# FFN 1 of a hybrid encoder layer: the gates' SwiGLU in two steps, two weight sums on VectorE, the bias table written by row pieces

## The chip, the cores and the metric

The kernel runs on one core of a Trainium2 chip. The metric is device time in microseconds, the median over executions of the whole kernel. The engines are named as the profile names them: PE is TensorE's matmul and PEld its weight load, DVE is VectorE, ACT is ScalarE, POOL is GpSimd, SP is SyncE, which here only issues DMAs. Each engine works through its own instructions in the order in which they were written; between engines semaphores hold an instruction back until what it reads is there, and until what it overwrites is no longer needed.

## What is computed

One layer, for 512 tokens of width 1024, in float32:

```python
f = swiglu(rms_norm(h, ffn1_pre_g), ffn1_w1, ffn1_w3, ffn1_w2)   # (silu(x @ w1) * (x @ w3)) @ w2, d_ff 2816
h = h + 0.5 * rms_norm(f, ffn1_post_g)
u = rms_norm(h, mix_pre_g)
q, k, v, xr, xg = split(u @ w_in)
y_a = (rg_lru(causal_conv(xr)) * gelu(xg)) @ w_lru_out           # recurrent branch
y_b = swa_sink_attention(q, k, v, sinks, bias) @ w_attn_out      # windowed attention, relative bias per head
h = h + rms_norm((g0 * y_a + g1 * y_b) @ w_o, mix_post_g)        # g = sigmoid(u @ w_gate + b_gate)
y = h + 0.5 * rms_norm(swiglu(rms_norm(h, ffn2_pre_g), ffn2_w1, ffn2_w3, ffn2_w2), ffn2_post_g)
```

The bias is one table of 32 buckets by 16 heads, spread over 383 relative positions. The change touches FFN 1, one helper that FFN 2 uses too, and the place where the bias table is prepared.

## The kernel before

**Numbers in two parts.** Every float32 operand of a matmul is split into a rounded part and a rest: `whi` by a ScalarE copy (line 193 or 158), `wlo` by a VectorE subtraction (line 194 or 159). A product is then three matmuls, hi by hi, lo by hi, hi by lo.

**FFN 1.** The activations are transposed, features on partitions, and held as `uT` (hi and lo). The two weight matrices w1a and w3a are cut into 22 tiles of 128 output features each. The first four gates (a gate is one w1a tile, its partner a w3a tile) are *single* tiles: `mm_feat` runs 24 matmuls of 512 columns into a whole PSUM bank. As the RMS scale of the input is not known early, FFN 1 multiplies with the unscaled input, and the gate is scaled afterwards by `Rb`, a row of factors per token. `swiglu(f)` does all of it in `silu_mul` (lines 430 to 439): VectorE multiplies the gate's bank by `Rb` (line 436), ScalarE takes the silu (437), VectorE multiplies by the partner's bank (438). Where these run is given by a small list of due points: `later(n, fn)` puts fn at the n-th `point()` from now, and a point comes every 12 matmuls; `point(True)` runs all that is left.

**Pairs.** The other 18 gates are taken two by two in a Winograd scheme (`class Pairs`): two weight tiles together are a 2 by 2 block matrix, the input likewise, and seven block products of 12 matmuls with 256 columns (`mm_s`, lines 475 to 477) do what eight would. A *job* is one such pair of tiles; jobs alternate between w1a (the gates) and w3a (their partners), 18 jobs in FFN 1 (n = 0 to 17) and 20 in FFN 2. Four weight sums S1 to S4 are needed per job. In `prep(m, 0)` GpSimd makes all four as additions of 128 by 512, `s12` (lines 521, 522) and `s34` (523, 524); for the very first two jobs VectorE makes them (argument `dve`). `prep(m, 1)` to `prep(m, 4)` split the raw tile, S1/S2, S3/S4 and the block a22.

**A job's order** (`run`, lines 538 to 608): product a11 into bank bu and copy q1 (554); s1 into bx and copy q5 (557); then `last()`, which is the seventh product a22 of the job before; `prep(n+1, 1)`; s2 added into bu and copy u (563); `prep(n+1, 2)`; a12 into bc and an addition (572); s4 added into bx and an addition (577); `prep(n+1, 3)`; s3 added into bu, copy v (581) and an addition (582); for a w3a job the products of gate and partner (587, 588); `prep(n+1, 4)`; `prep(n+2, 0)`; the loads for job n+3. In FFN 1 `last()` of a w1a job ends with a copy (596), the scaling by `Rb` (597) and the silu (598); of a w3a job with one product (605). In FFN 2 the input is scaled beforehand, so the silu is taken at once (600 to 602). In the last job the product a12 comes after v, and `tail()` runs ahead of it: it splits the first two hidden tiles and the first two tiles of w2a, the next matrix.

**Hooks.** `late` is a table (job, place): [functions], called after q1 (place 1), q5 (2) or u (3) of that job.

**Bias.** `bias_in` loads the one-hot matrix and the table by two GpSimd DMAs; `bias_rows` makes 16 rows (one a head) of 383 values with a matmul and a ScalarE copy into `erow`; `bias_spread(i)` writes to a scratch in DRAM 128 copies of each row of two heads, 383 KB, one DMA of GpSimd's queue, eight in all. The attention reads the scratch much later (line 1038).

**Memory.** All large tiles share 42 slots of 4 KB per partition. A load on SP's queue (line 143) waits until its slot's last reader is done.

Of the kernel before, what the change touches and what calls it, by code (L numbers as in the profile page):

```python
# [13 lines left out]
ALU = mybir.AluOpType  # L14
# [37 lines left out]
def hybrid_layer(ctx: ExitStack, tc: tile.TileContext, a: dict, out: bass.AP):  # L52
# [93 lines left out]
    def dma_to(n):  # L146
        while st["dma"] < min(n, len(order)):
            dma_one(st["dma"])
            st["dma"] += 1
# [277 lines left out]
        dma_to(st["split"] + 3)  # L427


    def silu_mul(ps1, ps3, R=None):  # L430

        t = slot([P, 2, SEQ], name="sw")
        if R is None:
            act.activation(t[:, 0, :], ps1, AF.Silu)
        else:
            dve.tensor_tensor(out=t[:, 0, :], in0=ps1, in1=R, op=ALU.mult)
            act.activation(t[:, 0, :], t[:, 0, :], AF.Silu)
        dve.tensor_tensor(out=t[:, 1, :], in0=ps3, in1=t[:, 0, :], op=ALU.mult)
        return t[:, 1, :]

# [39 lines left out]
    class Pairs:  # L480
# [14 lines left out]
        def prep(self, m, i, eng=None):  # L495
            if m >= len(self.jobs) or (m, i) in self.ready:
                return
            self.ready.add((m, i))
            k = self.k0 + 2 * m
            if i == 0:  # L500
                if k not in loaded or k + 1 not in loaded:
                    self.raws(m)
                s12, s34 = slot([P, 2 * QH], name="S12"), slot([P, 2 * QH], name="S34")
                self.w[m] = {"r": (raws.pop(k), raws.pop(k + 1)), "s": (s12, s34)}
            W = self.w[m]
            (ra, rb), (s12, s34) = W["r"], W["s"]
# [12 lines left out]
            if i == 0:  # L519
                e = eng or pool  # L520
                e.tensor_tensor(out=s12[:, :QH], in0=a21, in1=a22, op=ALU.add)
                e.tensor_tensor(out=s12[:, QH:], in0=s12[:, :QH], in1=a11, op=ALU.subtract)
                e.tensor_tensor(out=s34[:, QH:], in0=a12, in1=s12[:, QH:], op=ALU.subtract)
                e.tensor_tensor(out=s34[:, :QH], in0=a11, in1=a21, op=ALU.subtract)
            elif i == 1:
                halves(both(ra), "a11", "a12")
            elif i == 2:
                halves(both(s12), "s1", "s2")
            elif i == 3:
                halves(both(s34), "s3", "s4")  # L530
            elif i == 4:
                t = slot([P, 2, QH], F32R, name="w22")
                split2(t[:, 0, :], t[:, 1, :], a22)
                W["a22"] = t[:, 0, :], t[:, 1, :]
            if all((m, x) in self.ready for x in range(5)):
                del W["r"], W["s"]

        def run(self, tail, hooks={}):
            X = self.X
            assert st["get"] == st["split"] == self.k0, (st, self.k0)  # L540
            st["get"] = st["split"] = self.k0 + 2 * len(self.jobs)
            last = lambda: None
            for n, (nm, f) in enumerate(self.jobs):
                W = self.w.pop(n)
                first = nm == self.na
                tmp = slot([P, 4, 256], name="ct")
                q1, q5, u, v = (tmp[:, i, :] for i in range(4))
                c = slot([P, 2, SEQ], name="cc")
                if first:
                    self.c1[f] = c  # L550
                bu, bx, bc = (bank("c")[:, :256] for _ in range(3))
                at = lambda i: [f() for f in hooks.get((n, i), ())]
                mm_s(W["a11"], X["b11"], bu)
                act.activation(q1, bu, AF.Copy)  # L554
                at(1)
                mm_s(W["s1"], X["t1"], bx)
                act.activation(q5, bx, AF.Copy)
                at(2)
                last()
                self.prep(n + 1, 1)  # L560
                mm_s(W["s2"], X["t2"], bu, True)
                del W["s1"], W["s2"]
                act.activation(u, bu, AF.Copy)
                at(3)
                if n == len(self.jobs) - 1:
                    tail()
                self.prep(n + 1, 2)

                def c11():
                    mm_s(W["a12"], X["b21"], bc)  # L570
                    del W["a11"], W["a12"]
                    dve.tensor_tensor(out=c[:, 0, :256], in0=bc, in1=q1, op=ALU.add)

                if n < len(self.jobs) - 1:
                    c11()
                mm_s(W["s4"], X["b22"], bx, True)
                dve.tensor_tensor(out=c[:, 0, 256:], in0=bx, in1=u, op=ALU.add)
                self.prep(n + 1, 3)
                mm_s(W["s3"], X["t3"], bu, True)
                del W["s3"], W["s4"]  # L580
                act.activation(v, bu, AF.Copy)
                dve.tensor_tensor(out=c[:, 1, 256:], in0=v, in1=q5, op=ALU.add)
                if n == len(self.jobs) - 1:
                    c11()
                if not first:
                    c1 = self.c1[f]
                    dve.tensor_tensor(out=c1[:, 0, :], in0=c1[:, 0, :], in1=c[:, 0, :], op=ALU.mult)
                    dve.tensor_tensor(out=c1[:, 1, 256:], in0=c1[:, 1, 256:], in1=c[:, 1, 256:], op=ALU.mult)
                self.prep(n + 1, 4)
                self.prep(n + 2, 0)  # L590
                self.raws(n + 3)

                def last(W=W, bu=bu, c=c, f=f, first=first):
                    mm_s(W.pop("a22"), X["t4"], bu, True)
                    if first and self.R is not None:
                        act.activation(c[:, 1, :256], bu, AF.Copy)
                        dve.tensor_tensor(out=c, in0=c, in1=self.R, op=ALU.mult)  # L597
                        act.activation(c, c, AF.Silu)
                    elif first:
                        act.activation(c[:, 1, :256], bu, AF.Silu)  # L600
                        act.activation(c[:, 0, :], c[:, 0, :], AF.Silu)
                        act.activation(c[:, 1, 256:], c[:, 1, 256:], AF.Silu)
                    else:
                        c1 = self.c1.pop(f)
                        dve.tensor_tensor(out=c1[:, 1, :256], in0=bu, in1=c1[:, 1, :256], op=ALU.mult)
                        self.hid.f += [c1[:, 0, :], c1[:, 1, :]]

            last()
# [89 lines left out]
    def t_split(n):  # L698
        X1[f"t{n + 1}"] = to_slots(tg[n])
# [37 lines left out]
        act.activation(erow[0], pse[:N_HEADS, : NREL + 1], AF.Copy)  # L737

    def bias_spread(i):
        ev = erow[0][2 * i : 2 * i + 2, :NREL]  # L740
        pool.dma_start(out=scr[2 * i : 2 * i + 2], in_=bass.AP(tensor=ev.tensor, offset=ev.offset, ap=[ev.ap[0], [0, P], ev.ap[1]]))

# [45 lines left out]
    def single(nm, i, ahead):  # L788
        w = get(nm, i, ahead=ahead)
        ps.append(bank("f"))  # L790
        mm_feat(ps[-1], w)

    def swiglu(f):
        hid.f.append(silu_mul(ps[2 * f], ps[2 * f + 1], Rb[:, 0, :]))

    X1.update((b, uview(*q)) for b, q in (("b11", (0, 0)), ("b21", (1, 0)), ("b22", (1, 1))))
    P_ = pairs_a.prep
    for n, fn in (
        (1, lambda: t_sum(0)), (1, lambda: t_split(0)), (2, lambda: t_sum(1)),
        (3, lambda: P_(0, 0, dve)), (3, lambda: t_split(1)), (3, squares), (4, root),  # L800
        (5, lambda: P_(0, 1)), (5, lambda: t_sum(2)), (6, factor), (6, lambda: swiglu(0)), (6, lambda: dma_to(pairs_a.k0 + 4)),
        (7, lambda: t_sum(3)), (7, lambda: t_split(2)), (8, lambda: P_(0, 2)), (8, lambda: swiglu(1)),
        (9, lambda: P_(0, 3)), (9, lambda: P_(0, 4)), (10, lambda: t_split(3)), (10, lambda: swiglu(2)),
        (10, lambda: P_(1, 0, dve)),
    ):
        later(n, fn)
# [8 lines left out]
    point(True)  # L815
    xg.clear()
    tg.clear()
    swiglu(3)
    late = {(6, 1): [bias_in], (9, 1): [bias_rows]}

    def w2_ahead():
        hid.to(1)
# [467 lines left out]
```

## Time and profile before

| | us |
|---|---|
| median of 3 runs | 1169.75 (1169.62 to 1171.74) |
| the profiled execution | 1168.26 |
| its span, first to last instruction | 1166.2 |

| stretch of the span, us | what runs | length | PE busy | DVE busy | ACT busy | POOL busy | granted clock |
|---|---|---|---|---|---|---|---|
| 0 to 61 | FFN 1, single tiles | 61.0 | 51.67 | 43.36 | 39.34 | 6.16 | 0.96 |
| 61 to 251.3 | FFN 1, pairs | 190.3 | 184.38 | 156.54 | 97.17 | 118.77 | 0.99 |
| 251.3 to 367 | last product of the pairs, w2a | 115.7 | 102.49 | 55.48 | 44.26 | 2.19 | 0.94 |
| 367 to 834 | norms, projections, both branches, merge | 467.0 | 466.95 | 323.32 | 264.40 | 104.96 | 1.00 |
| 834 to 1039 | FFN 2, pairs | 205.0 | 205.00 | 168.50 | 112.63 | 127.93 | 1.00 |
| 1039 to 1166.2 | w2b, last norm, output | 127.2 | 120.51 | 52.25 | 37.70 | 0.56 | 0.98 |

How to read what follows. A timeline row gives the start in us from the span's beginning, the duration, the engine, the line, the operation, the tiles written and read, and in brackets how long the engine had been idle and what released it. A wait row gives who waited for whom, the total, how often, and the longest. A group row gives a count, the total busy time, the mean of one in ns, and the idle time before. A row of stretches gives for each engine its busy time and, after x, its number of instructions, then the granted TensorE clock (1.00 is full), the busy share of the 16 DMA engines, and GB/s.

### The profile page before, as it was taken

The page shows a single profiled execution, that of the slowest core. Times are in us where ns is not written, and L with a number is a line of the kernel's source. Part 1 is how long each engine was busy: PE and PEld are TensorE (multiplying, and loading weights), DVE is VectorE, ACT ScalarE, POOL GpSimd, SP SyncE. Part 2 cuts the span into 40 slices and gives each one's busy share as a digit, 9 for nine tenths or more (in the row PEclk, how much of TensorE's full clock was granted, in tenths as well). Part 3 has the DMA queues.
Part 4 walks back from the last instruction along what each step waited for, and adds up shares of the span by engine and source line. Part 5 has one row for each costly group of instructions (what it writes and reads, how often), then busy time and mean ns, then how long its engine had stood idle before and what let it go on. Part 6 is the DMA issues. An engine that isn't in the chain of part 4 may idle for free.

```text
span 1166.2 us, 17529 instructions
## 1 busy us (share of the span) xinstructions
PE 1131.0 (97%) x6835; PEld 1010.4 (87%) x6835; DVE 799.4 (69%) x1180; ACT 595.5 (51%) x1060; POOL 360.6 (31%) x275
## 2 busy tenths in 40 slices
PE   9889999969999999999999999999999999999997
PEld 7789999857888987788888888888999999998886
DVE  5868889845834765678586865767899778875313
ACT  7554554534523536983465654346555555564211
POOL 0046766530000000000455655000676557700000
PEclk9989999989999999999999999999999999999999
DMA  9213223279621521223332324360232333255101
GB/s 339 78 57 106 105 80 108 73 116 210 200 90 73 199 73 55 73 91 98 101 91 73 93 72 144 97 210 29 81 109 82 102 108 109 91 167 169 62 19 54
DMA packets 41873, 125.00 MB, mean 107 GB/s; under 512 B 9344, under 2 KB 11136, under 8 KB 41792
## 3 DMA queue, kind: packets, MB, share of 16 engines
q1 hardware_dynamic: 34272, 115.15, 29.9%
q0 software_dynamic: 7376, 8.49, 4.0%
q8 instruction: 53, 0.87, 0.3%
q10 hardware_dynamic: 144, 0.26, 0.1%
q14 instruction: 28, 0.23, 0.1%
HBM read 116.50 MB, written 7.33 MB: 106 GB/s over the span
## 4 chain that ended last, share of the span: by engine, by line
PE 80%; DVE 7%; DMA 5%; ACT 5%; issue 2%; SPq 0%; DVEq 0%; ACTq 0%
PE f L204 9%; PE f L203 9%; PE f L205 9%; PE c L475 8%; PE c L476 8%; PE c L477 8%; PE acc L223 8%; PE acc L221 8%; PE acc L222 8%; DVE wlo L194 3%; DMA raw_w2a<-in_w2a_dram 2%; ACT whi L193 1%; DVE cc L597 1%; PE pt L1093 1%; DMA raw_w3a<-in_w3a_dram 1%
## 5 line engine op out<-in xcount | busy, mean ns | idle before, releaser
L203 PE MATMUL f<-uT,whi 128*128 128x512 f32 (+1 forms) x472 | 171.9, 364 | 0.0
L204 PE MATMUL f<-uT,wlo 128*128 128x512 f32 (+1 forms) x472 | 170.7, 362 | 0.1
L205 PE MATMUL f<-uT,whi 128*128 128x512 f32 (+1 forms) x472 | 170.4, 361 | 0.0
L475 PE MATMUL c<-Xh,whi 128*128 128x256 f32 x456 | 131.0, 287 | 11.8 <-ACT ct L554 8.6
L223 PE MATMUL acc<-whi,hT 128*128 128x512 f32 x352 | 137.3, 390 | 0.3 <-DVE hT L194 0.3
L221 PE MATMUL acc<-whi,hT 128*128 128x512 f32 x352 | 137.5, 391 | 0.0
L222 PE MATMUL acc<-wlo,hT 128*128 128x512 f32 x352 | 137.1, 390 | 0.0
L476 PE MATMUL c<-Xh,wlo 128*128 128x256 f32 x456 | 130.3, 286 | 1.6 <-DVE wlo L194 1.6
L476 PE MATMUL c<-uT,wlo 128*128 128x256 f32 x456 | 129.8, 285 | 0.0
L475 PE MATMUL c<-uT,whi 128*128 128x256 f32 x456 | 129.8, 285 | 0.0
L477 PE MATMUL c<-Xl,whi 128*128 128x256 f32 x456 | 129.7, 285 | 0.0
L477 PE MATMUL c<-uT,whi 128*128 128x256 f32 x456 | 129.6, 284 | 0.0
L194 DVE TENSOR_TENSOR wlo<-S,whi 128x1024 fp32r<-128x1024 f32 x76 | 120.8, 1590 | 4.4 <-ACT whi L193 4.2
L203 PEld LDWEIGHTS f<-uT,whi 128*128 128x128 f32 x472 | 89.2, 189 | 14.5 <-issue 1.4
L204 PEld LDWEIGHTS f<-uT,wlo 128*128 128x128 f32 x472 | 89.3, 189 | 13.7 <-DVE wlo L159 0.9
L205 PEld LDWEIGHTS f<-uT,whi 128*128 128x128 f32 x472 | 89.2, 189 | 13.5
L475 PEld LDWEIGHTS c<-Xh,whi 128*128 128x128 f32 x456 | 88.0, 193 | 14.7 <-ACT ct L554 10.2
L476 PEld LDWEIGHTS c<-Xh,wlo 128*128 128x128 f32 x456 | 88.1, 193 | 2.6 <-DVE wlo L194 2.6
L476 PEld LDWEIGHTS c<-uT,wlo 128*128 128x128 f32 x456 | 88.2, 193 | 0.2 <-DVE wlo L194 0.2
L475 PEld LDWEIGHTS c<-uT,whi 128*128 128x128 f32 x456 | 88.2, 194 | 0.0
L477 PEld LDWEIGHTS c<-Xl,whi 128*128 128x128 f32 x456 | 88.1, 193 | 0.0
L477 PEld LDWEIGHTS c<-uT,whi 128*128 128x128 f32 x456 | 88.1, 193 | 0.0
(316 smaller groups left out, 2743.6 us busy)
## 6 DMA issues: line engine op xcount, KB each, us to landing
raw_w2a<-in_w2a_dram SPq DMA_DIRECT2D x22, 512.0 KB, 15.9
raw_w1b<-in_w1b_dram SPq DMA_DIRECT2D x22, 512.0 KB, 4.1
raw_w3b<-in_w3b_dram SPq DMA_DIRECT2D x22, 512.0 KB, 4.2
raw_w2b<-in_w2b_dram SPq DMA_DIRECT2D x22, 512.0 KB, 4.4
raw_w3a<-in_w3a_dram SPq DMA_DIRECT2D x21, 512.0 KB, 4.4
raw_w1a<-in_w1a_dram SPq DMA_DIRECT2D x20, 512.0 KB, 4.3
raw_wg<-in_wg_dram SPq DMA_DIRECT2D x16, 512.0 KB, 3.7
raw_xr<-in_xr_dram SPq DMA_DIRECT2D x8, 512.0 KB, 4.1
```

The source lines that it names most:

```text
L193: act.activation(hi, src, AF.Copy)
L194: dve.tensor_tensor(out=lo, in0=src, in1=f32(hi), op=ALU.subtract)
L203: pe.matmul(ps[:, c0:c1], wh[:, s], h_, start=k == 0, stop=False)
L204: pe.matmul(ps[:, c0:c1], wl[:, s], h_, start=False, stop=False)
L205: pe.matmul(ps[:, c0:c1], wh[:, s], l_, start=False, stop=k == KT - 1)
L221: pe.matmul(acc[n], x[:, 0, c], wh[:, s], start=first, stop=False)
L222: pe.matmul(acc[n], x[:, 0, c], wl[:, s], start=False, stop=False)
L223: pe.matmul(acc[n], x[:, 1, c], wh[:, s], start=False, stop=last)
L475: pe.matmul(ps, wh[:, s], xh, start=first, stop=False, skip_group_check=True)
L476: pe.matmul(ps, wl[:, s], xh, start=False, stop=False, skip_group_check=True)
L477: pe.matmul(ps, wh[:, s], xl, start=False, stop=k == 3, skip_group_check=True)
L597: dve.tensor_tensor(out=c, in0=c, in1=self.R, op=ALU.mult)
```

## The change

- `silu_mul` is cut in two. `gate(f)` does the scaling by `Rb` on VectorE, `swiglu(f)` the silu and the product. For gates 0 and 1 they stand one point apart (the scalings at points 6 and 7, the rest at 7 and 8). Gate 2 is scaled at point 10 and finished in job 0 after q1; gate 3, which stood ahead of the pairs, is scaled in job 0 after u and finished in job 1 after q1.
- In the pairs of FFN 1 `last()` no longer takes the silu of the scaled gates itself but hands it back, and `run` issues it ahead of the product s3: the products s2, a12 and s4 stand between.
- S3 and S4 are made by VectorE in `prep(m, 2)`, ahead of the split of S1/S2, in place of `prep(m, 0)`, where GpSimd (VectorE for the first two jobs) made them. This holds for both FFNs.
- `bias_in` moves from job 6 to job 1, `bias_rows` from job 9 to job 3. `bias_spread` writes 16 copies for all 16 heads in place of 128 copies for two heads, still 383 KB each and eight in all, and they move from points of the w2a product into jobs 4 to 11, one a job, after q1.

```diff
-    def silu_mul(ps1, ps3, R=None):
+    def silu_mul(ps1, ps3, t=None):
-        t = slot([P, 2, SEQ], name="sw")
-        if R is None:
-            act.activation(t[:, 0, :], ps1, AF.Silu)
-        else:
-            dve.tensor_tensor(out=t[:, 0, :], in0=ps1, in1=R, op=ALU.mult)
-            act.activation(t[:, 0, :], t[:, 0, :], AF.Silu)
+        t = t or slot([P, 2, SEQ], name="sw")
+        act.activation(t[:, 0, :], ps1, AF.Silu)
         dve.tensor_tensor(out=t[:, 1, :], in0=ps3, in1=t[:, 0, :], op=ALU.mult)
...
                 e.tensor_tensor(out=s12[:, QH:], in0=s12[:, :QH], in1=a11, op=ALU.subtract)
-                e.tensor_tensor(out=s34[:, QH:], in0=a12, in1=s12[:, QH:], op=ALU.subtract)
-                e.tensor_tensor(out=s34[:, :QH], in0=a11, in1=a21, op=ALU.subtract)
             elif i == 1:
                 halves(both(ra), "a11", "a12")
             elif i == 2:
+                dve.tensor_tensor(out=s34[:, QH:], in0=a12, in1=s12[:, QH:], op=ALU.subtract)
+                dve.tensor_tensor(out=s34[:, :QH], in0=a11, in1=a21, op=ALU.subtract)
                 halves(both(s12), "s1", "s2")
...
-                last()
+                silu = last() or silu
                 self.prep(n + 1, 1)
...
                 self.prep(n + 1, 3)
+                silu()
+                silu = lambda: None
                 mm_s(W["s3"], X["t3"], bu, True)
...
                         dve.tensor_tensor(out=c, in0=c, in1=self.R, op=ALU.mult)
-                        act.activation(c, c, AF.Silu)
-                    elif first:
+                        return lambda: act.activation(c, c, AF.Silu)
+                    if first:
...
-        ev = erow[0][2 * i : 2 * i + 2, :NREL]
-        pool.dma_start(out=scr[2 * i : 2 * i + 2], in_=bass.AP(tensor=ev.tensor, offset=ev.offset, ap=[ev.ap[0], [0, P], ev.ap[1]]))
+        ev, rows = erow[0][:, :NREL], slice(16 * i, 16 * i + 16)
+        pool.dma_start(out=scr[:, rows, :], in_=bass.AP(tensor=ev.tensor, offset=ev.offset, ap=[ev.ap[0], [0, 16], ev.ap[1]]))
...
+    gates = {}
+    def gate(f):
+        gates[f] = slot([P, 2, SEQ], name="sw")
+        dve.tensor_tensor(out=gates[f][:, 0, :], in0=ps[2 * f], in1=Rb[:, 0, :], op=ALU.mult)
     def swiglu(f):
-        hid.f.append(silu_mul(ps[2 * f], ps[2 * f + 1], Rb[:, 0, :]))
+        t = gates.pop(f)
+        hid.f.append(silu_mul(t[:, 0, :], ps[2 * f + 1], t))
...
-    swiglu(3)
-    late = {(6, 1): [bias_in], (9, 1): [bias_rows]}
+    late = {(0, 1): [lambda: swiglu(2)], (0, 3): [lambda: gate(3)], (1, 1): [bias_in, lambda: swiglu(3)], (3, 1): [bias_rows]}
+    for i in range(P // 16):
+        late[4 + i, 1] = [lambda i=i: bias_spread(i)]
...
-    for i in range(N_HEADS // 2):
-        later(4 + 3 * i, lambda i=i: bias_spread(i))
```

More of the change, by code (lines that the diff above doesn't have):

```diff
@@ L541, in run @@
             st["get"] = st["split"] = self.k0 + 2 * len(self.jobs)
-            last = lambda: None
+            last = silu = lambda: None
             for n, (nm, f) in enumerate(self.jobs):
@@ L800, in hybrid_layer @@
         (3, lambda: P_(0, 0, dve)), (3, lambda: t_split(1)), (3, squares), (4, root),
-        (5, lambda: P_(0, 1)), (5, lambda: t_sum(2)), (6, factor), (6, lambda: swiglu(0)), (6, lambda: dma_to(pairs_a.k0 + 4)),
-        (7, lambda: t_sum(3)), (7, lambda: t_split(2)), (8, lambda: P_(0, 2)), (8, lambda: swiglu(1)),
-        (9, lambda: P_(0, 3)), (9, lambda: P_(0, 4)), (10, lambda: t_split(3)), (10, lambda: swiglu(2)),
+        (5, lambda: P_(0, 1)), (5, lambda: t_sum(2)), (6, factor), (6, lambda: gate(0)), (7, lambda: swiglu(0)), (6, lambda: dma_to(pairs_a.k0 + 4)),
+        (7, lambda: t_sum(3)), (7, lambda: t_split(2)), (8, lambda: P_(0, 2)), (7, lambda: gate(1)), (8, lambda: swiglu(1)),
+        (9, lambda: P_(0, 3)), (9, lambda: P_(0, 4)), (10, lambda: t_split(3)), (10, lambda: gate(2)),
         (10, lambda: P_(1, 0, dve)),
```

## The prediction

> **What bounds the kernel now.** First the span, then TensorE's own waits, then the stretches around them, and last the engines that end them.
>
> ```profile
> core 0: 1166.2 us, clock 0.988
> ```
> ```profile
> PE 1131.0 (97%) x6835; PEld 1010.4 (87%) x6835; DVE 799.4 (69%) x1180; ACT 595.5 (51%) x1060; POOL 360.6 (31%) x275
> ```
> ```profile
> PE c L475 <- ACT ct L581: 12.9, 1, 12.9
> PE c L475 <- ACT ct L554: 8.6, 4, 7.6
> PE c L475 <- ACT ct L563: 3.3, 6, 1.2
> PE c L476 <- DVE wlo L194: 1.6, 5, 0.5
> ```
>
> TensorE is busy 97% of the span, so only its idle time can be won. Its longer waits (total, times, longest) all stand on the products of `mm_s`: two of 12.9 and 7.6 us, and a dozen short ones. A gap also costs clock, so each stretch is counted by its matmuls (x is their number; the last three columns are granted clock, DMA share and GB/s):
>
> ```profile
> 53.40:61.00 7.60, 0.09 (x1) 0.00 (x0) 6.14 (x8) 1.50 (x4) 5.33 (x4) 0.65 0.34 132
> 61.00:73.50 12.50, 12.42 (x85) 12.42 (x86) 5.94 (x8) 5.19 (x10) 3.23 (x3) 0.80 0.13 42
> 73.50:245.00 171.50, 165.88 (x1348) 162.11 (x1347) 147.08 (x144) 88.28 (x145) 115.54 (x68) 1.00 0.29 92
> 251.30:264.20 12.90, 0.07 (x1) 0.00 (x0) 0.45 (x2) 1.32 (x2) 0.00 (x0) 0.59 0.93 162
> 264.20:279.00 14.80, 14.42 (x62) 12.08 (x63) 6.53 (x11) 3.17 (x5) 1.07 (x1) 0.89 0.94 206
> 300.00:323.00 23.00, 23.00 (x103) 19.05 (x102) 18.48 (x20) 15.45 (x19) 0.00 (x0) 1.00 0.53 168
> 861.00:1029.00 168.00, 168.00 (x1403) 168.00 (x1402) 138.58 (x146) 90.22 (x158) 104.19 (x62) 1.00 0.30 100
> ```
>
> The FFN 2 pairs (last row) run without a gap: 168.00/1403 = 0.120 us for a matmul of 256 columns, so a job of 84 takes 10.06. From 300 to 323 one of 512 columns takes 23.00/103 = 0.223. Against these rates FFN 1 loses time in three places:
> - start of the pairs: 7.6 idle, then 85 matmuls in 12.5 where 10.2 would do, 2.3 more at a clock of 0.80. Together 9.9.
> - 16 jobs from 73.5 to 245: 171.5 less 1346 × 0.1197 = 161.1, and less an estimated 1.0 for the two other matmuls (the bias rows): 9.4.
> - end of the pairs: 12.9 idle, then 12 + 50 matmuls in 14.8 where 1.4 + 11.2 would do, 2.2 more at 0.89. Together 15.1.
>
> That is 34.4 us, all that can be won here. The Trainium skill (TensorE: Matmul & The Clock Gate, "Part 1: The HAM clock gate") puts the time at half clock after a restart at about 3.4 us, an estimated 1.7 lost each time. These rows show 2.3 and 2.2; by the page the 34.4 would be 1.1 less.
>
> **Start: the gates' SwiGLU.** ScalarE, then VectorE, then GpSimd before the 7.6 us wait ends (start, duration, line, tiles, idle before):
>
> ```profile
> 53.48 0.63 ACT L437 ACTIVATE sw<-sw 128x512 f32<-128x512 f32 x1 [2.16 <-DVE sw L436]
> 60.13 0.63 ACT L437 ACTIVATE sw<-sw 128x512 f32<-128x512 f32 x1 [6.02 <-DVE sw L436]
> 60.66 0.36 ACT L554 ACTIVATE ct<-c 128x256 f32<-128x256 f32 x1
> ```
> ```profile
> 49.88 1.22 DVE L194 TENSOR_TENSOR wlo<-S,whi 128x1024 fp32r<-128x1024 f32 x1 [0.26 <-ACT whi L193]
> ...
> 54.75 0.68 DVE L521 TENSOR_TENSOR S<-raw_w3a 128x512 f32<-128x512 f32 x1
> 55.46 0.69 DVE L522 TENSOR_TENSOR S<-S,raw_w3a 128x512 f32<-128x512 f32 x1
> 56.19 1.63 DVE L523 TENSOR_TENSOR S<-raw_w3a,S 128x512 f32<-128x512 f32 x1
> 57.75 1.74 DVE L524 TENSOR_TENSOR S<-raw_w3a,raw_w3a 128x512 f32<-128x512 f32 x1
> 59.41 0.68 DVE L436 TENSOR_TENSOR sw<-f,Rb 128x512 f32<-128x512 f32 x1
> ```
> ```profile
> 55.52 1.76 POOL L521 TENSOR_TENSOR S<-raw_w1a 128x512 f32<-128x512 f32 x1 [54.07 <-DVE S L521]
> ```
>
> Job 0's third product adds into bank bu, so it waits for the copy q1 (L554). On ScalarE that copy stands behind gate 3's silu, which waits for its scaling (59.41), which stands on VectorE behind the four adds for job 1. The change puts q1 ahead: gate 2's silu comes behind q1, gate 3's scaling behind u, its silu behind q1 of job 1. Of the four adds two stay here. So q1 runs when its product ends and the 9.9 go. What is late next is job 1's second product, which needs wlo of S1/S2. VectorE's queue to it, from 53.45 (where the scaling ends that releases the silu of 53.48): two adds 0.68 + 0.69, the SwiGLU product 0.69, wlo of the raw tile 1.22, gate 3's scaling 0.68, S4 and S3 1.37, wlo 1.22: 60.0, and with GpSimd's two adds alongside (1.63 and 1.74 against 0.68 shows about 1 us per collision) up to 62. TensorE asks for it five products (four of job 0, one of job 1, 12 × 0.12 = 1.44 each) after 53.4, at 60.6. So the new wait is between 0 and 1.5; I take 1.5, since GpSimd's row at 55.52 falls right among VectorE's. **Term: 8.4 won**, bounds 5 (another pair of collided adds, 3.4, in front) and 9.9.
>
> **The pairs' silu and S3/S4.** VectorE's groups from 73.5 to 245, and ScalarE's silu:
>
> ```profile
> L194 DVE TENSOR_TENSOR wlo<-S,whi 128x1024 fp32r<-128x1024 f32 x32 | 54.0, 1688 | 0.9 <-ACT whi L193 0.9
> L582 DVE TENSOR_TENSOR cc<-ct 128x256 f32<-128x256 f32 x16 | 19.8, 1237 | 0.0
> ...
> L572 DVE TENSOR_TENSOR cc<-c,ct 128x256 f32<-128x256 f32 x16 | 6.6, 414 | 0.0
> ```
> ```profile
> L598 ACT ACTIVATE cc<-cc 128x1024 f32<-128x1024 f32 x8 | 8.5, 1060 | 15.1 <-DVE cc L597 15.1
> ```
>
> Every second job ScalarE stands idle 15.1/8 = 1.9 us for the scaling L597, then does 1.06 of silu, with the next weights' whi and the copy u queued behind it; hence the waits on L563 (3.3) and on wlo (1.6). With the silu three products later both orders are free: 4.9 won. The rest of the 9.4 stays, among it 1.0 on L554 (8.6 − 7.6).
>
> Against this VectorE takes two adds a job: 2 × 0.69 = 1.38 if alone, 1.63 + 1.74 = 3.37 if GpSimd is in the way. It also gets relief, since GpSimd's adds halve: wlo takes 1.69 against 1.22 alone, L582 1.24 against 0.41 for the same shape in L572, so collisions cost 15.0 + 13.2 us in these two groups, 1.8 a job; half is 0.9. Net +0.5 on 147.08/16 = 9.2 a job, under the 10.06. What is queued behind: ScalarE's whi of S3/S4 now waits for VectorE's adds, and behind it the deferred silu, the copy v and the next q1. v is needed only two products (2.9 us) after S3 ends, so I charge 0.5 over the whole stretch, bounds 0 and 13 (in half the jobs the adds at 3.37 with this relief: 9.2 + 2.5 = 11.7, 1.6 over, 8 times). **Term: 4.4 won**, bounds 8 lost and 9.4 won. FFN 2 has the same two adds, and its silu is not scaled, so it is not deferred: 138.58/16.7 = 8.3 a job plus 0.5, still under 10.06, so nothing; bound 7 lost (8.3 + 2.5 = 10.8, 0.7 over, in half of 20 jobs). If VectorE's slack there were gone, all of the 1.38 would show in each job.
>
> On GpSimd two adds and, in eight jobs, one DMA issue are left in place of four adds. On SP's queue a load waits for a free slot, and the raw tiles are now held until VectorE's adds have read them, behind wlo of the same job instead of the job before; the loads keep a job's lead, so I charge nothing.
>
> **The end: the bias table's writes.** ScalarE around the long wait, then GpSimd's issues, then landing times (min, median, max) of the bias writes and of the w2a loads, then a load that GpSimd issues:
>
> ```profile
> 246.86 1.06 ACT L598 ACTIVATE cc<-cc 128x1024 f32<-128x1024 f32 x1 [1.29 <-DVE cc L597]
> 247.83 0.36 ACT L563 ACTIVATE ct<-c 128x256 f32<-128x256 f32 x1
> 248.09 0.62 ACT L193 ACTIVATE hT<-sw 128x512 fp32r<-128x512 f32 x1
> 248.61 1.05 ACT L158 ACTIVATE whi<-raw_w2a 128x1024 fp32r<-128x1024 f32 x1
> 249.56 0.62 ACT L193 ACTIVATE hT<-sw 128x512 fp32r<-128x512 f32 x1
> 262.88 1.06 ACT L158 ACTIVATE whi<-raw_w2a 128x1024 fp32r<-128x1024 f32 x1 [12.70 <-DMA raw_w2a<-in_w2a_dram]
> 263.84 0.36 ACT L581 ACTIVATE ct<-c 128x256 f32<-128x256 f32 x1
> ```
> ```profile
> 237.07 7.42 POOL L741 DMA_DIRECT2D bias_scr<-erow  x7
> ```
> ```profile
> DMA to landing us min/median/max: 27.9/43.2/47.8
> ```
> ```profile
> DMA to landing us min/median/max: 3.6/15.9/31.3
> ```
> ```profile
> bc_ffn_post_g<-in_ffn_post_g_dram POOLq DMA_DIRECT2D x2, 512.0 KB, 4.2
> ```
>
> The copy v (L581) frees the bank for the last a22 product, and waits behind the second whi of w2a, whose load came late: seven bias writes were issued just before, and while they ran w2a loads took a median 15.9 us where 3.6 is possible. With the writes in jobs 4 to 11 the load is there in time. ScalarE then has this queue without the silu of 246.86 in front, which comes behind it: the row of 249.56 ends at 250.2 − 1.06 = 249.1, the second whi at 250.2, the silu at 251.3 and v at 251.6. TensorE comes free at 251.3, so 0.3 is left; I charge 0.6. **Term: 14.5 won**, bounds 10 (a load that starts one landing of 4.2 too late) and 15.1.
>
> Where they go, the eight writes meet the pairs' loads, at a DMA share of 0.29. Each moves 383 KB, and none landed in under 27.9 us from 2 source partitions. From 16, its price lies between that and the 4.2 of a 512 KB load on the same queue; eight times the source rows puts it near the latter, well inside a job of 10.06. The raw tiles have a job's lead over it, so nothing shows: 0 lost here, and the dear end of the price is a rival below. The Trainium skill (DMA: Bandwidth & Descriptors, "Why a DMA increments its semaphore by 16 and not by 1") says that a copy runs on the largest number of engines up to 16 that divides the outer dimensions of both sides: 2 before, 16 after, an estimated 27.9 × 2/16 = 3.5 us. By the page too the loss is 0. The issues (1.06 each on GpSimd), the two loads and the bias rows only move.
>
> **Sum.** 8.4 + 4.4 + 14.5 = 27.3. The profiled execution took 1168.26 us (span 1166.2 and 2.1 around it), so 1141.0; the median of the runs is 1.5 above it, so I forecast 1142 (1138 to 1147).
>
> **Rivals.**
> - All three losses go: 1168.3 − 34.4 + 1.5 = 1135.4. For it: FFN 2 pairs have no gap with the same work. Against: FFN 1 has the scaling besides.
> - The pairs win nothing, the start half: 5 + 14.5 − 1 = 18.5, so 1151. For it: VectorE's 9.2 of 10.06 leaves little room, and every wlo of S pays for a collision (1.69 against 1.22).
> - The long wait stays, because w2a's loads lacked slots rather than bandwidth: 1142 + 14.5 = 1156 to 1157. Against: DMA share 0.93 in that very row.
> - Slower: VectorE becomes the bound. Adds at 3.37 without relief make 12.6 a job in FFN 1 and 11.7 in FFN 2, so 18 × 2.5 + 20 × 1.6 = 77 over the 1135.4: 1212. It decides for a loss from a net 2.2 us a job on (8.7 mean to 10.06, and 34.4/38 more); I expect 0.5.
> - Slower: the bias writes stay at 27.9 us among the pairs' loads. At w2a's 15.9 for loads with a lead of 10.7 (171.5/16) eight jobs lose 5 each, 40 on the forecast: 1182. It decides from a landing above the lead, 10.7.
>
> **Numbers.** Forecast 0.50, all gone 0.15, pairs win nothing 0.20, wait stays 0.05, VectorE bound 0.03, bias writes 0.03, other new waits, from 1154 up to a small loss, 0.04. Range: the first three, 1134 to 1154. 0.2% (2.3 us) is about what runs can tell from no change: faster 0.92 (the first four and half of the last), within 0.2% 0.02, slower 0.06.
>
> **What would show it.** Right: no gap of 7 us after job 0's second product, the first L437 in the pairs behind an L554; bias_scr landing in about 4 us and raw_w1a unchanged; w2a landing near 4; VectorE's wlo of S below 1.69; FFN 2 pairs without gaps. Wrong: waits of TensorE on L563, L581 or wlo of over 1 us in most jobs (the adds' place), raw tiles landing above 10 us, or a time above 1154.

## The result, and the profile after

| | us | runs | ratio to before, with 95% interval |
|---|---|---|---|
| before, in the same set | 1170.63 | 1169.62 to 1171.74 | |
| changed kernel | 1136.91 | 1136.39 to 1137.54 | 0.9712 [0.9695, 0.9729] |
| its profiled execution | 1137.54 | span 1135.5 | |

The kernel is 2.9% faster. The time lies inside the range of 1134 to 1154, but under the 1138 to 1147 that the likeliest case had to itself: it stands 1.5 from the rival "all three losses go" and 5.1 from the forecast.

The cores, the busy times and TensorE's waits on other engines' results (total, times, longest) of the changed kernel:

```profile
core 0: 1135.5 us, clock 0.998
```
```profile
PE 1125.4 (99%) x6835; PEld 1006.0 (89%) x6835; DVE 790.0 (70%) x1252; ACT 597.8 (53%) x1060; POOL 241.1 (21%) x203
```
```profile
PE c L472 <- DVE wlo L194: 0.6, 1, 0.6
PE c L471 <- ACT ct L579: 0.3, 1, 0.3
```

Of the waits on `mm_s` (now lines 471 to 473) the 12.9, 7.6, 3.3 and 1.6 us of before are gone; 0.6 and 0.3 are left. The granted clock rose from 0.988 to 0.998: the pairs now read 1.00 from their start, where the two stretches behind the long gaps read 0.80 and 0.89 before. The stretches that answer to the pairs of FFN 1 and FFN 2 before, with the same columns:

```profile
62.10:233.00 170.90, 170.52 (x1408) 168.93 (x1409) 152.24 (x185) 93.40 (x153) 67.20 (x38) 1.00 0.47 117
...
820.00:988.00 168.00, 168.00 (x1401) 167.84 (x1400) 129.96 (x172) 92.19 (x158) 58.76 (x32) 1.00 0.31 98
```

Counted as in the prediction: in the pairs 170.90, less 1406 × 0.1199 = 168.6 (0.1199 is 168.00/1401, the second row), less an estimated 1.0 for the bias rows' two matmuls, leaves 1.3 lost, where it was 9.4. At the end only the wait on the copy v (now L579) is lost, 0.3 where it was 15.1. At the start these rows of TensorE show the one wait that is left:

```profile
61.06 0.28 PE L471 MATMUL c<-Xh,whi 128*128 128x256 f32 x1
61.93 0.39 PE L472 MATMUL c<-Xh,wlo 128*128 128x256 f32 x1 [0.59 <-DVE wlo L194]
```

From one matmul to the next 0.87 in place of 0.12: about 0.8 lost, where it was 9.9. Together 34.4 fell to 2.4, so 32.0 were won. The two spans differ by 1166.2 − 1135.5 = 30.7. Of the 1.3 between them 0.6 is in the FFN 2 pairs, by the first and last start of their L475 (before) and L471 (after):

```profile
L475 PE MATMUL c<-uT,whi x240: 282/284/284, 838.0 to 1037.8; 128*128 128x256 f32 x120
```
```profile
L471 PE MATMUL c<-uT,whi x240: 283/283/283, 806.4 to 1006.8; 128*128 128x256 f32 x120
```

That is 199.8 before and 200.4 after. The runs below show where it comes from: the same count gives 200.3 or 200.4 in b_s34, a_silu_now, a_late_place and a_two_heads, in which VectorE makes S3 and S4 beside GpSimd's S1 and S2, and 199.8 in b_bias, b_gate, b_silu, a_s34_pool, a_mixed and a_all_dve, in which one engine makes all four in FFN 2. The other 0.7 was not followed.

### The profile page after: what moved, and what is told of

Its sections match the earlier page's. It is cut to its first block, busy times and chain, and to the rows that moved or that the text cites. A ratio compares the mean times of both kernels' runs of the same rounds, so it can differ in the third digit from the quotient of the medians.

```text
span 1135.5 us, 17456 instructions
## 1 busy us (share of the span) xinstructions
PE 1125.4 (99%) x6835; PEld 1006.0 (89%) x6835; DVE 790.0 (70%) x1252; ACT 597.8 (53%) x1060; POOL 241.1 (21%) x203
## 4 chain that ended last, share of the span: by engine, by line
PE 91%; DVE 5%; ACT 3%; issue 1%; DMA 0%; SPq 0%; DVEq 0%; ACTq 0%
PE c L472 10%; PE f L203 10%; PE f L204 10%; PE f L205 10%; PE c L473 10%; PE c L471 10%; PE acc L222 8%; PE acc L223 8%; PE acc L221 8%; DVE wlo L194 2%; PE pt L1097 1%; PE s L1061 1%; PE s L1060 1%; DVE S L523 1%; PE tr L313 1%
## 5 line engine op out<-in xcount | busy, mean ns | idle before, releaser
L471 PE MATMUL c<-Xh,whi 128*128 128x256 f32 x456 | 129.1, 283 | 0.0
L471 PE MATMUL c<-uT,whi 128*128 128x256 f32 x456 | 129.0, 283 | 0.0
L193 ACT ACTIVATE whi<-S 128x1024 fp32r<-128x1024 f32 x76 | 80.2, 1057 | 53.0 <-DVE S L523 53.0
L194 DVE TENSOR_TENSOR wlo<-S,whi 128x1024 fp32r<-128x1024 f32 x76 | 101.9, 1341 | 0.3 <-ACT whi L193 0.3
L203 PEld LDWEIGHTS f<-uT,whi 128*128 128x128 f32 x472 | 89.1, 189 | 14.5 <-issue 1.4
L204 PEld LDWEIGHTS f<-uT,wlo 128*128 128x128 f32 x472 | 89.2, 189 | 13.8 <-DVE wlo L159 0.9
L471 PEld LDWEIGHTS c<-Xh,whi 128*128 128x128 f32 x456 | 87.5, 192 | 0.6 <-ACT ct L550 0.6
L471 PEld LDWEIGHTS c<-uT,whi 128*128 128x128 f32 x456 | 87.5, 192 | 0.0
```

Of the source, the lines that this page charges most:

```text
L193: act.activation(hi, src, AF.Copy)
L194: dve.tensor_tensor(out=lo, in0=src, in1=f32(hi), op=ALU.subtract)
L203: pe.matmul(ps[:, c0:c1], wh[:, s], h_, start=k == 0, stop=False)
L204: pe.matmul(ps[:, c0:c1], wl[:, s], h_, start=False, stop=False)
L471: pe.matmul(ps, wh[:, s], xh, start=first, stop=False, skip_group_check=True)
```

## The experiments

### Each part alone

The change has four parts that can be made one at a time on the kernel before: the bias table's writes, the gates' SwiGLU in two steps, the pairs' silu, and the sums S3 and S4.

```diff
# b_bias: bias_in, bias_rows and bias_spread as in the changed kernel, nothing else
-        ev = erow[0][2 * i : 2 * i + 2, :NREL]
+        ev, rows = erow[0][:, :NREL], slice(16 * i, 16 * i + 16)
...
+        late[4 + i, 1] = [lambda i=i: bias_spread(i)]
```

> The kernel before with the bias part alone (row pieces, jobs 4 to 11). Theory, the bias writes starve the w2a loads and nothing else at the end of the pairs: TensorE's wait of 12.9 us on the copy v and its clock cost go, some 14.6 us, so 1156; the 7.6 us wait at the start and the short ones in the pairs stay; w2a lands in about 4.4 us. Rival, w2a's loads lacked slots: the long wait stays, 1169 to 1171.

Measured: 1152.68 against 1169.16 before, ratio 0.9861 [0.9846, 0.9876], 16.5 us won. TensorE's waits on the pairs' products, and w2a's loads with their median landing at the end of the row:

```profile
PE c L475 <- ACT ct L554: 8.9, 1, 8.9
PE c L476 <- DVE wlo L194: 3.5, 8, 1.1
PE c L475 <- ACT ct L563: 1.5, 4, 0.5
```
```profile
raw_w2a<-in_w2a_dram SPq DMA_DIRECT2D x22, 512.0 KB, 4.3
```

The 12.9 us wait on the copy v is gone, w2a lands in a median 4.3 where it took 15.9, and the two other losses stay. So w2a's loads did not lack slots. The 15.1 that were counted for the end lie inside the interval, which is 14.5 to 18.0 us.

```diff
# b_gate: gate(f) and swiglu(f) as in the changed kernel, nothing else
...
-    swiglu(3)
-    late = {(6, 1): [bias_in], (9, 1): [bias_rows]}
+    late = {(0, 1): [lambda: swiglu(2)], (0, 3): [lambda: gate(3)], (1, 1): [lambda: swiglu(3)], (6, 1): [bias_in], (9, 1): [bias_rows]}
```

> The kernel before with the gates' SwiGLU in two steps alone; S3 and S4 of job 1 still stand on VectorE ahead of it. Theory, the 7.6 us wait is q1 behind the silu on ScalarE: it goes though VectorE's four adds stay, 1161 to 1163. Rival, the adds themselves are what is late: a wait of 3 to 5 us comes a product later, 1165 to 1168.

Measured: 1158.66, ratio 0.9916 [0.9899, 0.9933], 10.5 us won. Its waits:

```profile
PE c L471 <- ACT ct L577: 12.8, 1, 12.8
PE c L471 <- ACT ct L559: 2.6, 5, 1.2
PE c L472 <- DVE wlo L194: 1.9, 6, 0.5
...
PE c L471 <- ACT ct L550: 1.0, 3, 0.3
```

The 7.6 us wait on q1 (L550 here) is gone; what is left on that line is the 1.0 of the later jobs. No wait longer than 1.2 takes its place, so the whole 9.9 is won (the interval is 7.8 to 11.8). That is more than the expectation's 6 to 8, which had the wait of 7.6 but not the 2.3 that the prediction counted behind it.

```diff
# b_silu: the silu of a scaled pair of gates ahead of s3 in place of behind its scaling
-                last()
+                silu = last() or silu
...
+                silu()
+                silu = lambda: None
...
-                        act.activation(c, c, AF.Silu)
+                        return lambda: act.activation(c, c, AF.Silu)
```

> The kernel before with the pairs' silu three products later alone. Theory, ScalarE's order: TensorE's waits on u (L563 before, 3.3 us) and on wlo (1.6) go, 4 to 5 us, 1166. Rival, VectorE's collisions with GpSimd set those waits: under 2 us, 1169 to 1171.

Measured: 1160.48, ratio 0.9927 [0.9910, 0.9943], 8.7 us won (6.7 to 10.5), where the prediction's sum had 4.9 for the silu and the expectation 4 to 5. TensorE's long waits on the pairs' products, and a stretch of 158 us of the pairs:

```profile
PE c L475 <- ACT ct L583: 13.8, 1, 13.8
PE c L475 <- ACT ct L554: 7.4, 1, 7.4
```
```profile
73.00:231.00 158.00, 158.00 (x1313) 157.23 (x1313) 148.16 (x141) 88.26 (x141) 112.27 (x65) 1.00 0.32 98
```

Of the waits in the pairs only the two long ones are left, and between them TensorE runs without a gap at its full rate, 158.00/1313 = 0.120 us. The silu's place alone was the cause of all that the pairs lost, also of what the wait rows had put on L554 and of the short gaps that no row named. How it reaches that far shows in one job of w1a, first before, then with the silu deferred:

```profile
95.06 2.01 DVE L597 TENSOR_TENSOR cc<-cc,Rb 128x1024 f32<-128x1024 f32 x1 [1.74 <-ACT cc L596]
...
97.10 1.06 ACT L598 ACTIVATE cc<-cc 128x1024 f32<-128x1024 f32 x1 [2.07 <-DVE cc L597]
98.06 1.04 ACT L193 ACTIVATE whi<-raw_w1a 128x1024 fp32r<-128x1024 f32 x1
...
99.01 0.36 ACT L563 ACTIVATE ct<-c 128x256 f32<-128x256 f32 x1
99.14 1.52 DVE L194 TENSOR_TENSOR wlo<-raw_w1a,whi 128x1024 fp32r<-128x1024 f32 x1 [2.08 <-ACT whi L193]
```
```profile
93.70 1.05 ACT L193 ACTIVATE whi<-raw_w1a 128x1024 fp32r<-128x1024 f32 x1
93.84 2.00 DVE L599 TENSOR_TENSOR cc<-cc,Rb 128x1024 f32<-128x1024 f32 x1 [2.00 <-ACT cc L598]
...
94.86 0.39 ACT L563 ACTIVATE ct<-c 128x256 f32<-128x256 f32 x1
...
95.77 2.32 DVE L194 TENSOR_TENSOR wlo<-raw_w1a,whi 128x1024 fp32r<-128x1024 f32 x1
```

Before, ScalarE waits 2.07 for the scaling and then takes the silu, and only then makes whi of the raw tile; so VectorE in its turn stands idle 2.08 from the end of its scaling until that whi is there. With the silu moved, whi is made while VectorE scales, u is copied 1 us after the scaling's start and not 4 us, and wlo follows the scaling at once. VectorE's groups say the same for the whole stretch from 73 to 231 (last columns: busy time, mean ns, idle time before), before and then with the deferred silu:

```profile
L194 DVE TENSOR_TENSOR wlo<-raw_w1a,whi 128x1024 fp32r<-128x1024 f32 x8 | 11.0, 1378 | 16.6 <-ACT whi L193 16.6
```
```profile
L194 DVE TENSOR_TENSOR wlo<-raw_w1a,whi 128x1024 fp32r<-128x1024 f32 x8 | 13.0, 1631 | 0.0
```

16.6 us of VectorE's time in eight jobs, 2.1 each, had been lost to an order on ScalarE. The two kernels below that keep the old order keep this idle time too, 16.6 us in b_s34 and 14.5 in a_silu_now (seven jobs in the stretch), and TensorE's waits with it.

```diff
# b_s34: S3 and S4 by VectorE, in prep(m, 2), nothing else
-                e.tensor_tensor(out=s34[:, QH:], in0=a12, in1=s12[:, QH:], op=ALU.subtract)
-                e.tensor_tensor(out=s34[:, :QH], in0=a11, in1=a21, op=ALU.subtract)
...
+                dve.tensor_tensor(out=s34[:, QH:], in0=a12, in1=s12[:, QH:], op=ALU.subtract)
+                dve.tensor_tensor(out=s34[:, :QH], in0=a11, in1=a21, op=ALU.subtract)
```

> The kernel before with S3 and S4 on VectorE alone. Theory of relief: the collisions with GpSimd halve, wlo of S falls from 1.69 to about 1.40 us, the pairs win 3 to 5 us and the start 3 to 4 since two adds fewer stand ahead of gate 3's scaling: 1162 to 1165. Rival, VectorE is near its bound and the adds cost: the pairs lose as much as the start wins or more, 1170 or above.

Measured, in ten runs: 1169.26, ratio 0.9998 [0.9988, 1.0007]: no change. The relief came as expected (wlo of S takes a mean of 1.40 us between 73 and 231, before 1.72), but not the 4 to 7 us that it was to win. The waits on the pairs' products, beside the two long ones, which stay:

```profile
PE c L476 <- DVE wlo L194: 5.6, 5, 1.5
...
PE c L475 <- ACT ct L563: 0.7, 2, 0.5
```

The waits on u (L563) shrink from 3.3 to 0.7 (why was not followed), but those on wlo grow from 1.6 to 5.6: the two adds now stand in VectorE's queue between the late wlo of the raw tile and the wlo that the next product needs. In one such job that late wlo starts at 139.86 after 2.07 of waiting for whi, the adds take 141.26 to 143.6, wlo of S1/S2 starts at 143.56, and TensorE waits 1.40 until 144.82.

The four gains are 16.5 + 10.5 + 8.7 − 0.1 = 35.6, the whole change won 33.7 in the set of the result and 32.7 in a later one, so the parts add up nearly and none hides another.

### One part undone in the changed kernel

```diff
# a_silu_now: the silu behind the scaling again
...
-                        return lambda: act.activation(c, c, AF.Silu)
+                        act.activation(c, c, AF.Silu)
...
```

> The kernel after with the pairs' silu right behind its scaling again. Theory, ScalarE's order matters even without half of the collisions: TensorE waits on u some 0.5 us in every second job, 4 to 5 us, 1141 to 1142. Rival, fewer collisions alone empty the pairs: 1137 to 1138.

Measured: 1145.06 against 1169.06 before, ratio 0.9793 [0.9779, 0.9808], 8.3 us more than the changed kernel (the mean of its two medians, 1136.74). Its waits:

```profile
PE c L472 <- DVE wlo L194: 7.2, 7, 1.5
```

This is the relief from collisions without the deferred silu. It wins nothing in the pairs, and TensorE waits seven times for wlo (7.2) and only twice for u (0.7), where the expectation had u.

```diff
# a_s34_pool: S3 and S4 on GpSimd in prep(m, 0) again
+                e.tensor_tensor(out=s34[:, QH:], in0=a12, in1=s12[:, QH:], op=ALU.subtract)
+                e.tensor_tensor(out=s34[:, :QH], in0=a11, in1=a21, op=ALU.subtract)
...
-                dve.tensor_tensor(out=s34[:, QH:], in0=a12, in1=s12[:, QH:], op=ALU.subtract)
-                dve.tensor_tensor(out=s34[:, :QH], in0=a11, in1=a21, op=ALU.subtract)
```

> The kernel after with S3 and S4 back on GpSimd in prep 0 (on VectorE for the first two jobs). Theory, the relief from collisions is what emptied the pairs of waits together with the silu: 3 to 5 us lost in the pairs and 1 to 3 at the start, 1141 to 1145. Rival, the deferred silu alone does it: 1137 to 1139.

Measured: 1134.77 (1134.34 to 1137.02), ratio 0.9709 [0.9695, 0.9724]. Without the move the kernel is not slower, against both expectations, which were 1137 to 1145; three of its four runs lie under every run of the changed kernel, and it is the lowest time of all. What the move does to VectorE shows in the same stretch of four kernels: before, b_s34, a_s34_pool, and the changed kernel (third pair of numbers: VectorE; fifth: GpSimd).

```profile
73.00:231.00 158.00, 152.71 (x1240) 149.15 (x1239) 134.56 (x131) 82.54 (x135) 102.70 (x58) 1.00 0.29 94
```
```profile
73.00:231.00 158.00, 151.75 (x1244) 149.35 (x1243) 128.32 (x159) 82.69 (x133) 53.44 (x30) 1.00 0.29 94
```
```profile
73.00:231.00 158.00, 158.00 (x1313) 157.23 (x1313) 147.04 (x143) 87.20 (x142) 109.92 (x64) 1.00 0.49 121
```
```profile
73.00:231.00 158.00, 157.62 (x1302) 156.03 (x1301) 139.80 (x170) 86.03 (x143) 63.75 (x36) 1.00 0.47 116
```

Counted by wlo of S, which comes twice a job, these rows hold 14.5, 14.5, 15.5 and 15.5 jobs. The first has two additions of 0.4 us over, the third three instructions of the end of the pairs, some 2.5 us. Without these VectorE is busy 9.2 us a job before and 8.85 in b_s34, 9.3 with GpSimd's sums and 9.0 in the changed kernel. Two more adds a job make VectorE's time 0.3 to 0.4 *shorter*: the relief from collisions is larger than the adds. That it is GpSimd which stretches them shows in wlo of S over the whole kernel, with four, two and no sums on GpSimd (before, the changed kernel, and a_all_dve below):

```profile
L194 DVE TENSOR_TENSOR wlo<-S,whi 128x1024 fp32r<-128x1024 f32 x76 | 120.8, 1590 | 4.4 <-ACT whi L193 4.2
```
```profile
L194 DVE TENSOR_TENSOR wlo<-S,whi 128x1024 fp32r<-128x1024 f32 x76 | 101.9, 1341 | 0.3 <-ACT whi L193 0.3
```
```profile
L194 DVE TENSOR_TENSOR wlo<-S,whi 128x1024 fp32r<-128x1024 f32 x76 | 92.5, 1218 | 1.1 <-ACT whi L193 0.8
```

With the silu deferred neither value holds TensorE up in the pairs: TensorE's only listed wait on wlo is 0.5 in a_s34_pool (at 71 us) and 0.6 in the changed kernel (at 62), both ahead of this stretch.

Two more variants of the same question ran beside a second set of the changed kernel:

```diff
# a_mixed: as a_s34_pool, but the first two jobs' S3 and S4 stay where the change put them
+                W["soon"] = eng is None
+                if W["soon"]:
...
+                if not W["soon"]:
...
```
```diff
# a_all_dve: S1 and S2 by VectorE too
-                e = eng or pool
+                e = dve
```

> The kernel after as it is, on the same chip as the three beside it: 1136 to 1138. It is the measure for the next one.

> The kernel after, with S3 and S4 made by GpSimd in prep 0 again except for the first two jobs of FFN 1, where VectorE makes them in prep 2. Theory, the deferred silu alone empties the pairs and the adds' engine is of no weight there: 1134 to 1136, with none of the 0.25 us waits on wlo that the kernel after shows in every second job. Rival, GpSimd's four adds cost VectorE the same time in collisions: 1137 to 1139.

> The kernel after with S1 and S2 on VectorE too, in prep 0, so GpSimd adds nothing. VectorE is busy 181 of 185 us in the pairs of FFN 1 after. Theory, that busy time is stretched by collisions that now vanish: it stays near 180, 1136 to 1140. Rival, VectorE is at its bound: two more adds of 0.68 us in 18 jobs make 24 us, up to 1160.

Measured beside 1169.31 before: the changed kernel 1136.57 (1136.10 to 1137.19), ratio 0.9720 [0.9706, 0.9735]; a_mixed 1135.94 (1135.67 to 1136.04), 0.9714 [0.9700, 0.9729]; a_all_dve 1139.50 (1138.21 to 1140.32), 0.9744 [0.9729, 0.9758]. By these intervals neither a_mixed nor a_s34_pool is proven a better version than the changed kernel. Of a_s34_pool's 2 us 0.6 have a place in the profile, the FFN 2 pairs (199.8 against 200.4, see the result).

With all four sums VectorE does not become the bound either. The expectation's "181 of 185 us" is not VectorE's time: in 185.2 us from 51 on the changed kernel's weight loads (PEld) are busy 181.9 and VectorE 166.4. In a_all_dve VectorE is busy 132.7 of the 158 us from 73 on, in 15 jobs, so 8.85 a job, less than with two sums on GpSimd. All that comes is two waits on wlo, of which the longer is

```profile
113.43 0.39 PE L472 MATMUL c<-uT,wlo 128*128 128x256 f32 x1 [2.80 <-DVE wlo L194]
```

The time that the adds take is not its cause. This wlo stands on VectorE behind the sums of a w1a tile, and they wait 7.59 us for that tile's load, which takes 22.3 us to land. As GpSimd has no sums to do between the bias writes, it issues all eight within 4 us (82.3 to 86.3), and they take a median 19.7 and up to 32.1 to land; from 84 to 118 the DMA share is 0.97, in the changed kernel 0.56. So the 2.8 us that a_all_dve is slower fit the bunched writes; the same kernel with the writes spread out was not run.

### Place and shape of the bias writes

```diff
# a_late_place: the changed kernel's writes at the points of the w2a product, as before
-    for i in range(P // 16):
-        late[4 + i, 1] = [lambda i=i: bias_spread(i)]
...
+    for i in range(N_HEADS // 2):
+        later(4 + 3 * i, lambda i=i: bias_spread(i))
```

> The kernel after with the new row pieces, but issued at the old points of the w2a product (GpSimd, free then, issues all of them at the end of the pairs). Theory, the shape is what helps: a write lands in 6 us or a little more, w2a stays under 10 us, 1137 to 1139. Rival, the 3 MB themselves are in w2a's way: TensorE waits 3 to 10 us at the end of the pairs, 1141 to 1149.

Measured: 1150.58, ratio 0.9842 [0.9825, 0.9858]: 13.8 above the changed kernel (here and below, the mean 1136.74 of its two medians). TensorE's wait, who waits for w2a, and the writes:

```profile
PE c L471 <- ACT ct L579: 12.3, 1, 12.3
```
```profile
ACT whi L158 <- DMA raw_w2a<-in_w2a_dram: 19.2, 5, 11.9
```
```profile
L739 POOL DMA_DIRECT2D bias_scr<-erow x8: 563/563/587, 217.0 to 220.9; - x8
...
DMA to landing us min/median/max: 5.8/18.8/31.7
```

Eight writes issued within 4 us, all ahead of w2a, take until 220.9 + 31.7 = 252.6, some 35 us for all eight. In the wide shape too they are in w2a's way, and the same copy v waits about as long as before, more than either expectation had. The place is worth about 14 us. With it goes the spacing, as in the new place GpSimd issues one write a job; the two were not told apart. What the shape alone is worth in the old place was not run: the kernel before less the 10.5, 8.7 and −0.1 of the other parts would be 1150.0, so next to nothing if the parts add.

```diff
# a_two_heads: the changed kernel's place, the old shape: 128 copies of two heads
-        ev, rows = erow[0][:, :NREL], slice(16 * i, 16 * i + 16)
+        ev = erow[0][2 * i : 2 * i + 2, :NREL]
...
# a_four_heads: 64 copies of four heads
+        g, rows = slice(4 * (i // 2), 4 * (i // 2) + 4), slice(64 * (i % 2), 64 * (i % 2) + 64)
+        ev = erow[0][g, :NREL]
...
```

> The kernel after, but each bias write again 128 copies for two heads, in jobs 4 to 11 as after. Theory, a write from two source rows is narrow: each lands in about 28 us or more, three are in flight at a time, the pairs' loads take 8 to 16 us instead of 4.4, and TensorE waits where their lead of a job runs out: 1140 to 1180. Rival, only the place matters and the pairs have bandwidth to spare: 1137, loads under 8 us.

> The kernel after, with bias writes of 64 copies for four heads each, still 383 KB and one a job in jobs 4 to 11. Theory, a write goes as fast as its source rows are many (25 us from 2, 4.2 us a write from 16 where eight of them follow each other): some 14 to 18 us from 4, the pairs' loads 8 to 14 us, TensorE's waits under 5 us: 1137 to 1142. Rival, any narrow write costs what the two rows did, 1150 to 1156.

Measured: two heads 1156.26, ratio 0.9897 [0.9878, 0.9916]; four heads 1161.55, 0.9937 [0.9913, 0.9961]. So the shape is worth 19.5 us in the new place, and four heads (24.8) are no better than two, against both expectations, which ended at 1156. First the changed kernel's writes and w1a loads (of which the last number is the median landing), then those with two heads, then with four:

```profile
DMA to landing us min/median/max: 5.6/5.9/6.6
...
raw_w1a<-in_w1a_dram SPq DMA_DIRECT2D x20, 512.0 KB, 4.3
```
```profile
DMA to landing us min/median/max: 22.3/25.4/35.6
...
raw_w1a<-in_w1a_dram SPq DMA_DIRECT2D x20, 512.0 KB, 10.2
```
```profile
DMA to landing us min/median/max: 19.4/23.6/29.5
...
raw_w1a<-in_w1a_dram SPq DMA_DIRECT2D x20, 512.0 KB, 10.4
```

The narrow writes are issued 13 and 14 us apart on average, so two or so are in flight at a time. How early it hurts show the first write of two heads, which is issued at 90.6 and lands in 22.3, and the two w3a loads issued 7 and 8 us behind it:

```profile
L143 SPq DMA_DIRECT2D raw_w3a<-in_w3a_dram x2: 328/639/950, 97.5 to 98.8; - x2
...
DMA to landing us min/median/max: 14.5/14.8/15.1
```

These loads land in 14.5 and 15.1, where the changed kernel's take a median 4.5. The wait reaches TensorE: in the kernel with four heads ScalarE waits 11.60 us for a w1a load until 185.14, makes whi of it, then copies u, for which TensorE stands idle:

```profile
186.52 0.58 PE L471 MATMUL c<-Xh,whi 128*128 128x256 f32 x1 [9.08 <-ACT ct L559]
```

My theory that the landing goes as one over the number of source rows fell: from 2 to 4 rows the first write's went from 22.3 to 22.2 and the median from 25.4 to 23.6; from 4 to 16 the median went from 23.6 to 5.9. The rule of the Trainium skill (DMA: Bandwidth & Descriptors, "Why a DMA increments its semaphore by 16 and not by 1") that a copy uses the largest number of engines up to 16 that divides both outer dimensions gives 2, 4 and 16 engines. If the landing went as one over that number, the 27.9 of before would give an estimated 14 for four heads and 3.5 for sixteen; the runs show 19.4 at the least and 5.6 at the least. The rule on the number of engines can still hold; it is the step from engines to time that the runs do not bear out. What sets the time of a write with few source rows stays open.

## Why the prediction was right, and where not

The time fell inside the range, but the likeliest case, with a chance of 0.50, was not the one that came: the rival "all three losses go", with 0.15, was nearer.

- **What bounds the kernel** (34.4 us at three places) was right: 32.0 of it went, and nothing else moved by more than 1 us.
- **Start, 8.4 won:** 9.1. The new wait on wlo for job 1's second product came, at the line and for the reason given: the wlo that it waits for had collided (1.22 alone):

```profile
59.55 2.33 DVE L194 TENSOR_TENSOR wlo<-S,whi 128x1024 fp32r<-128x1024 f32 x1
```

  It was 0.8, where the prediction took 1.5, the upper end of 0 to 1.5.
- **Pairs, 4.4 won:** 8.1, and 8.7 for the deferred silu alone. This is the mis-sized term and most of the miss. The sum took 4.9 for the silu from the two wait rows that its queue explained, L563 and wlo, and left "the rest of the 9.4", among it the 1.0 on L554, as of another cause. The run of that part alone has no gap left at all. A late whi on ScalarE made VectorE stand idle 2.1 us in every second job, and what stood behind it on VectorE came later too. By which of these steps each of TensorE's gaps came was not followed. The row was there to be read: 16.6 us of VectorE's idle time on one group, ended by ScalarE.
- **S3 and S4, a charge of 0.5 in the pairs, nothing in FFN 2:** right in effect (0 to 2 us of loss over the kernel, 0.6 of it in FFN 2) and wrong in its working. The sum had two adds of 0.69 less a relief of 0.9, net +0.5 on VectorE's 9.2 a job; measured −0.3 to −0.4. By the group rows of b_s34 against before (73 to 231, 14.5 jobs) the adds took 1.7 a job, as they collide too, and the older instructions became 1.9 shorter. Of this 1.1 is in wlo of S and L582, where the prediction had half of 1.8, and 0.8 in groups that it left out, as L587 (before, then b_s34, 73 to 235):

```profile
L587 DVE TENSOR_TENSOR cc<-cc,cc 128x512 f32<-128x512 f32 x8 | 8.7, 1087 | 0.0
```
```profile
L587 DVE TENSOR_TENSOR cc<-cc,cc 128x512 f32<-128x512 f32 x8 | 5.4, 680 | 0.0
```

  The step that failed is that collisions were counted "in these two groups" alone.
- **End, 14.5 won:** 14.8; b_bias alone wins 16.5. The copy v waits 0.3 in place of 0.6.
- **Bias writes, "landing in about 4 us":** 5.9. That is half as much again, with no effect, since it is still under the lead of 10.7. Charging nothing for them among the pairs' loads was right: raw_w1a lands in 4.3 as before. It rests on one write a job: issued together, as in a_all_dve, they do hold a load up.
- **Rivals.** "All three losses go" at 1135.4 came nearest. "VectorE becomes the bound" is far off: with four adds a job VectorE is busy 8.85 us of a job, and the 2.8 us lost there follow a late load. "The long wait stays" was wrong for this kernel, where the writes are gone from that place, but a_late_place shows the wait needs only the wide writes there. "Bias writes stay at 27.9" is right as a mechanism and too dear: two heads landed in a median 25.4, over the lead of 10.7 as the rival asked, and the kernel then took 1156.3, a loss of 19.5 and not of 40.
- **The sum:** 27.3 put the profiled execution at 1141.0, it took 1137.5. The 3.5 are 3.7 from the pairs, 0.7 from the start and 0.3 from the end, less the 0.6 of FFN 2 and the 0.7 that was not followed, within rounding. One reading is too simple: of the 2.2 put to the clock behind the second long gap, the granted 0.89 over 14.8 us gives 1.6. The forecast added 1.5 for the median over the profiled execution; here the median is 0.6 under it.

## What to carry to other kernels

An activation that waits for another engine's result holds up everything behind it on its own engine; the cost is not in the wait rows of that one consumer but in the idle time of every engine whose inputs come later, so look for one idle row with a large sum and one releaser before splitting a stage's loss into causes. A transfer that must not disturb others should be looked at for its place, its spacing and its shape: here the new place with two source rows left the kernel 20 us slower than with sixteen, and sixteen rows in the old place, all at once, 14 us slower. Work that moves between two engines which collide should be priced with the collisions that it ends, and then asked whether the receiving engine sets any time at all.

## What was not expected of the hardware

- Two more adds of 128 by 512 a job made VectorE's busy time 0.3 to 0.4 us a job shorter, as GpSimd ran two fewer beside it (9.3 to 9.0, and 9.2 to 8.85). With no sums on GpSimd wlo of S took 1.22 us, with all four 1.59.
- One 383 KB write from two or four source rows on GpSimd's queue raised the median landing of 512 KB loads on SP's queue from 4.3 to 10.2 and 10.4, though only one such write was issued a job, 13 to 14 us apart on average.
- The landing of such a write hardly depends on whether it has 2 or 4 source rows (a median of 25.4 and 23.6), and with 16 it is 5.9.
